# Rotary tables and softplus built before the input block arrives, and the sum of squares accumulated by TensorE, in a two-layer hybrid trunk

## The chip, the cores and the metric

One of the eight cores of a Trainium2 chip runs the whole program. The metric is the device time of one execution in microseconds; lower is better. Where an engine is named, PE is TensorE, DVE is VectorE, ACT is ScalarE, POOL is GpSimd and SP is SyncE, which here only issues transfers.

## The reference

Two layers over a sequence of 256 positions and 1024 channels. What the change touches is the start of a layer and three small things that depend on no activation:

```python
def rmsnorm(x, g):
    y = xf * lax.rsqrt(jnp.mean(xf * xf, axis=-1, keepdims=True) + EPS)
    return (y * g.astype(jnp.float32)).astype(x.dtype)
...
mod = c_act @ ada_w + ada_b
shift, scale, gate = jnp.split(mod, 3, axis=-1)
h = rmsnorm(x, norm_g) * (1.0 + scale[:, None]) + shift[:, None]
z = h @ w_in
...
log_a = -LRU_C * r * jax.nn.softplus(-lam.astype(jnp.float32))
...
ang = pos.astype(jnp.float32)[:, :, None] * inv
cos, sin = jnp.cos(ang), jnp.sin(ang)
...
q = rope(rmsnorm(b_q.reshape(shp), qn_g[:, None, :]), pos) * (HEAD_DIM ** -0.5)
k = rope(rmsnorm(b_k.reshape(shp), kn_g[:, None, :]), pos)
```

So h needs the whole of x (for the mean of squares) and the modulation vectors; the cosines and sines need only positions and a list of frequencies, and softplus only a parameter vector.

## The kernel before

The activations stay in SBUF. The weights are streamed: each layer is a list of units of 384 to 512 KB, and `load_next` issues one transfer per unit from SP's queue into one of six `raw` buffers. ACT copies a unit to the reduced-precision tile `whi` (L223), DVE makes the remainder `wlo` (L224), and PE forms three products per block: whi by the high part of h, wlo by it, and whi by the low part of h (L789 to L791 and L777 to L779 for the first units, L797 to L799 for the others). There are four `whi` and four `wlo` buffers.

At the start of layer 0 the modulation matrix also streams in, as sixteen tiles of 512 KB (`ada_...` and some `raw`). DVE reduces each of them against `crow`, the conditioning row spread over all partitions (L325). `crow` itself is made on the way: DVE computes `cact` from `c` and puts it on the diagonal of eight blocks (`diag`, L309), PE multiplies these by a matrix of ones (L313), ACT copies the result from PSUM (L314).

The statistics of x go as follows. `stats_start` squares x on ACT in four pieces (L372); DVE adds the four pieces to one (L375, L376); PE multiplies the two halves of that by ones (L379), which sums over partitions. `rstd_full` takes the logarithm on ACT (L341), the exponential of minus one half of it (L345), and refines that on DVE (L346 to L348). Then, for each of eight channel tiles j, DVE forms `tmp` (L357), ACT the high part `hhi` (L359) and DVE the low part `hlo` (L360).

The first sixteen units of a layer (q, k and v of the first pair of heads, and the gate bg, four each) are computed as one group; the prediction calls this the first group. Its results stay in PSUM until DVE and ACT have read them: for q and k, L552, L554 and L556 for each of two halves t. After it come units of one column block, the first of them ax and ag in turn (L797 to L799), which need the PSUM buffers that q and k have filled.

The order of instructions on each engine is set when the program is built, by a scheduler that takes the dependences, the order of the code and its own estimate of durations; `issue_after` adds a dependence by hand. Once built, every engine executes its own list strictly in order. Each activation function belongs to a table that ACT must have loaded; where the next one needs another table, the build puts a load of it ahead (ACT_TABLE_LOAD). L301 asks by hand for a table that holds both logarithm and exponential.

Of the kernel before, what the change touches and what calls it, by code (L numbers as in the profile page):

```python
# [10 lines left out]
F32 = mybir.dt.float32  # L11
# [3 lines left out]
ALU = mybir.AluOpType  # L15
# [3 lines left out]
D, S, L, P = 1024, 256, 2, 128  # L19
# [107 lines left out]
def hybrid_trunk(ctx: ExitStack, tc: tile.TileContext, ws, ada, vec, gates, a2, qkg, c_t, x_t, pos, inv, eye,  # L127
# [109 lines left out]
    SY.dma_start(out=c_sb, in_=c_t)  # L237
    SY.dma_start(out=eye_sb, in_=eye)
    for i in range(2):
        SY.dma_start(out=x_sb[:, 4 * i:4 * i + 4], in_=x_t[:, 4 * i:4 * i + 4])  # L240
    SY.dma_start(out=vec_sb, in_=vec)

# [20 lines left out]
    att_sb = one.tile([P, 3, P], F32, name="att_sb")  # L263
    G.memset(att_sb, 0.0)

    def load_after(key, *pairs):
# [101 lines left out]
    def stats_start():  # L368
        sq = []
        for i, tag in enumerate(("cv", "csg", "co", "bv")):  # L370
            t = two.tile([P, 2, S], F32, name="sq", tag=tag, bufs=1 if i < 3 else 2)
            A.activation(t, x_sb[:, 2 * i:2 * i + 2], AF.Square)  # L372
            sq.append(t)
            if i % 2:
                V.tensor_tensor(sq[i - 1], sq[i - 1], t, ALU.add)  # L375
        V.tensor_tensor(sq[0], sq[0], sq[2], ALU.add)  # L376
        ps = xps()
        for j in range(2):
            T.matmul(ps[:, 0:S], ones, sq[0][:, j], start=(j == 0), stop=(j == 1))  # L379
        return ps  # L380
# [50 lines left out]
    def rope_tables(l):  # L431
        gq = two.tile([P, 2, 3, 64], F32, name="gq", tag="pr", bufs=2)
        load_after(None if l else ("sy", "a", 7), (gq, qkg[l].partition_broadcast(P)))
        ct = one.tile([P, 2, 2, 3, 64], F32, name="ctab", tag="ctab")
# [514 lines left out]


    sts = stats_start()
    rstd = rstd_full(sts)
# [3 lines left out]

    def tables():
        a, v = cur["h_last"]
        with tc.issue_after(a), tc.issue_after(v):
            load_after(("sy", "a", 3), (pos_sb, pos), (inv_sb, inv.partition_broadcast(P)))  # L960
            angles()
            rope_tables(0)

    def small():
        a, v = cur["h_last"]
        with tc.issue_after(a), tc.issue_after(v):
            softplus()
        V.tensor_scalar(vec_sb[:, :, V_ON:V_ON + 2], vec_sb[:, :, V_ON:V_ON + 2], 0.5, None, ALU.mult)

    sts = layer(0, h, {2: tables, 15: load_small, 16: small})  # L970


# [98 lines left out]
```

## Time and profile before

| what | us |
|---|---|
| three runs | 910.75, 912.31, 912.46 |
| median | 912.31 |
| profiled execution | 912.47 |
| its span, first to last instruction | 910.7 |

The profiled execution lies 0.16 us above the median, and 1.8 us of its time lie outside the span. In the span PE is busy 96%, DVE 74%, ACT 58% and POOL 19%. All times below are microseconds from the start of the span. The start of the program is another regime than the rest: PE first gets to the layer's products at 20.41 us.

### The profile page before, as it was taken

Reading aid. Unit: us, or ns where it says so; the run is one execution under the profiler, and the core shown is the slowest. Engines: PE = TensorE matmul, PEld = TensorE weight load, DVE = VectorE, ACT = ScalarE, POOL = GpSimd, SP = SyncE. Lnnn points to the kernel's source line nnn. Section 1 sums busy time; section 2 is a strip of 40 time slices with the busy share of each in tenths; the row PEclk is TensorE's granted clock in tenths of the full one; section 3 lists DMA queues with packets and bytes.
Section 4 is the critical chain, followed back from the end, with each engine's and each line's share of the span. In section 5 each row is a group of like instructions: output and inputs, shape, how many; then the busy total and the mean of one; then the engine's idle time right before and its main releaser. Section 6 shows DMA issues by size and latency. Waiting matters only on the chain.

```text
span 910.7 us, 16407 instructions
## 1 busy us (share of the span) xinstructions
PE 872.9 (96%) x6340; PEld 825.3 (91%) x6340; DVE 673.0 (74%) x1115; ACT 532.0 (58%) x897; POOL 175.1 (19%) x160
## 2 busy tenths in 40 slices
PE   3989999999999999999999999989999999999998
PEld 3978999999988888999889999989999988899998
DVE  6998898669666667666775888986896666656674
ACT  4376976686644554634454689666874545554451
POOL 0026365124000110100030525551330001000000
PEclk9999999999999999999999999999999999999999
DMA  9884456446765666676655544563667565455651
GB/s 328 317 279 139 145 165 207 132 136 201 240 189 191 202 212 205 208 238 206 224 152 160 177 145 145 179 195 109 190 206 232 160 190 163 150 173 185 188 163 47
DMA packets 52111, 170.16 MB, mean 187 GB/s; under 512 B 6240, under 2 KB 8160, under 8 KB 52032
## 3 DMA queue, kind: packets, MB, share of 16 engines
q1 hardware_dynamic: 51216, 167.04, 57.7%
q10 hardware_dynamic: 672, 1.87, 0.7%
q8 instruction: 50, 0.82, 0.4%
q0 software_dynamic: 144, 0.20, 0.2%
q14 instruction: 29, 0.24, 0.1%
HBM read 168.23 MB, written 1.05 MB: 186 GB/s over the span
## 4 chain that ended last, share of the span: by engine, by line
PE 57%; DVE 18%; DMA 10%; issue 7%; ACT 5%; POOL 3%; SPq 0%; DVEq 0%; ACTq 0%
PE mm L797 10%; PE mm L799 10%; PE mm L798 10%; DMA raw<-in_ada_dram 8%; DVE wlo L224 7%; PE mm L791 6%; PE mm L790 6%; PE mm L789 6%; PE xps L172 1%; ACT whi L223 1%; POOL ss L560 1%; PE xps L168 1%; DVE raw L325 1%; DVE rb L554 1%; DVE ra L552 1%
## 5 line engine op out<-in xcount | busy, mean ns | idle before, releaser
L224 DVE TENSOR_TENSOR wlo<-raw,whi 128x1024 fp32r<-128x1024 f32 (+2 forms) x288 | 335.6, 1173 | 86.9 <-ACT whi L223 85.5
L223 ACT CAST whi<-raw 128x1024 fp32r<-128x1024 f32 (+2 forms) x288 | 280.2, 977 | 189.5 <-PE mm L798 123.6
L797 PE MATMUL mm<-hhi,whi 128*128 128x256 f32 x768 | 217.8, 284 | 3.3 <-DVE rb L554 3.2
L799 PE MATMUL mm<-hhi,wlo 128*128 128x256 f32 x768 | 216.6, 282 | 3.1 <-DVE wlo L224 3.1
L798 PE MATMUL mm<-hlo,whi 128*128 128x256 f32 x768 | 216.0, 281 | 0.0
L789 PE MATMUL mm<-whi,hhi 128*128 128x384 f32 (+2 forms) x480 | 170.9, 361 | 7.2 <-ACT hhi L359 6.5
L790 PE MATMUL mm<-wlo,hhi 128*128 128x384 f32 (+2 forms) x480 | 173.0, 362 | 1.4 <-DVE wlo L224 1.2
L791 PE MATMUL mm<-whi,hlo 128*128 128x384 f32 (+2 forms) x480 | 169.1, 358 | 0.5 <-DVE hlo L360 0.5
L797 PEld LDWEIGHTS mm<-hhi,whi 128*128 128x128 f32 x768 | 144.6, 188 | 5.3 <-ACT tmp L847 3.6
L799 PEld LDWEIGHTS mm<-hhi,wlo 128*128 128x128 f32 x768 | 144.5, 188 | 4.3 <-DVE wlo L224 3.7
L798 PEld LDWEIGHTS mm<-hlo,whi 128*128 128x128 f32 x768 | 144.8, 189 | 0.4
L789 PEld LDWEIGHTS mm<-whi,hhi 128*128 128x128 f32 x480 | 93.4, 195 | 15.3 <-ACT hhi L359 7.9
L790 PEld LDWEIGHTS mm<-wlo,hhi 128*128 128x128 f32 x480 | 93.9, 196 | 9.1 <-DVE wlo L224 2.8
L325 DVE CUSTOM_DVE_ANT_0 raw<-raw,crow,vec_sb 128x1024 f32<-128x1024 f32 x38 | 48.7, 1283 | 70.7 <-DMA raw<-in_ada_dram 70.7
L791 PEld LDWEIGHTS mm<-whi,hlo 128*128 128x128 f32 x480 | 92.7, 194 | 7.2 <-DVE hlo L360 0.8
L797 PE MATMUL mm<-yhi,whi 128*128 128x256 f32 x320 | 89.9, 281 | 2.1 <-DVE mg L939 2.1
L798 PE MATMUL mm<-ylo,whi 128*128 128x256 f32 x320 | 89.3, 279 | 0.0
L799 PE MATMUL mm<-yhi,wlo 128*128 128x256 f32 x320 | 89.2, 279 | 0.0
L797 PEld LDWEIGHTS mm<-yhi,whi 128*128 128x128 f32 x320 | 60.4, 189 | 3.1 <-DVE mg L939 2.3
L799 PEld LDWEIGHTS mm<-yhi,wlo 128*128 128x128 f32 x320 | 60.2, 188 | 0.8 <-DVE mrg L905 0.8
L798 PEld LDWEIGHTS mm<-ylo,whi 128*128 128x128 f32 x320 | 60.1, 188 | 0.0
L698 POOL TENSOR_TENSOR at_hl<-att_sb,at_hl 128x384 fp32r<-128x384 f32 x8 | 8.8, 1096 | 207.1 <-ACT at_hl L697 207.1
(236 smaller groups left out, 1408.0 us busy)
## 6 DMA issues: line engine op xcount, KB each, us to landing
raw<-in_ws_dram SPq DMA_DIRECT2D x192, 512.0 KB, 4.0
raw<-in_ws_dram SPq DMA_DIRECT2D x88, 384.0 KB, 3.2
raw<-in_ada_dram SPq DMA_DIRECT2D x38, 512.0 KB, 4.5
raw<-in_ws_dram SPq DMA_DIRECT2D x8, 400.0 KB, 5.4
g_raw<-in_gates_dram ACTq DMA_DIRECT2D x3, 512.0 KB, 4.9
x_sb<-in_x_t_dram SPq DMA_DIRECT2D x2, 512.0 KB, 6.7
ada_yhi<-in_ada_dram SPq DMA_DIRECT2D x2, 512.0 KB, 7.9
ada_ylo<-in_ada_dram SPq DMA_DIRECT2D x2, 512.0 KB, 9.1
```

Source lines behind the costliest of these rows:

```text
L168: seen[0] = T.matmul(*a, **k).ins
L172: seen[0] = T.transpose(*a, **k).ins
L223: A.copy(hi, r)
L224: V.tensor_tensor(lo, r, hi.bitcast(F32), ALU.subtract)
L325: V.tensor_tensor_reduce(w, w, crow2, 1.0, b, ALU.mult, ALU.add, a if i == 0 else m)
L552: V.tensor_tensor(ra.rearrange("p (g s) d -> p g s d", g=3), z4, ctab[l][:, i, t].unsqueeze(2).to_broadcast(bc), ALU.mult)
L789: T.matmul(o, ah, wh, start=(k == 0), stop=False)
L790: T.matmul(o, ah, wl, start=False, stop=False)
L791: T.matmul(o, al, wh, start=False, stop=(k == KT - 1))
L797: T.matmul(ps[:, 0:S], hi[:, a:b], xh[:, k], start=(k == 0), stop=False)
L798: T.matmul(ps[:, 0:S], hi[:, a:b], xl[:, k], start=False, stop=False)
L799: T.matmul(ps[:, 0:S], lo[:, a:b], xh[:, k], start=False, stop=(k == nk - 1))
```

## The change

The sum of squares loses its three additions on DVE; PE accumulates eight products instead of two. Positions, frequencies and the gains of layer 0 (`g0`, a tile that shares the buffer of `pt1`) are loaded from ACT's queue at the very start, and no longer from SP's queue among the weights; the parameter vector `vec` is loaded ahead of x. `angles`, `rope_tables(0)`, `softplus` and the halving of one parameter stand in the code ahead of `stats_start`; before, they were held behind the h tiles by `issue_after`.

```diff
--- before.py
+++ after.py
@@ -236,9 +236,9 @@
     inv_sb = one.tile([P, 32], F32, name="inv_sb")
     SY.dma_start(out=c_sb, in_=c_t)
     SY.dma_start(out=eye_sb, in_=eye)
+    SY.dma_start(out=vec_sb, in_=vec)
     for i in range(2):
         SY.dma_start(out=x_sb[:, 4 * i:4 * i + 4], in_=x_t[:, 4 * i:4 * i + 4])
-    SY.dma_start(out=vec_sb, in_=vec)
 
     tiles = []
     for tag, n in (("yhi", 2), ("ylo", 2), ("hraw", 2), ("ya", 1), ("sga", 1), ("la", 1), ("big2", 1)):
@@ -262,6 +262,10 @@
     V.memset(hpi, float(np.pi / 2))
     att_sb = one.tile([P, 3, P], F32, name="att_sb")
     G.memset(att_sb, 0.0)
+
+    g0 = one.tile([P, 2, 3, 64], F32, name="g0", tag="pt1")
+    for t, s in ((pos_sb, pos), (inv_sb, inv.partition_broadcast(P)), (g0, qkg[0].partition_broadcast(P))):
+        A.dma_start(out=t, in_=s)
 
     def load_after(key, *pairs):
 
@@ -371,12 +375,9 @@
             t = two.tile([P, 2, S], F32, name="sq", tag=tag, bufs=1 if i < 3 else 2)
             A.activation(t, x_sb[:, 2 * i:2 * i + 2], AF.Square)
             sq.append(t)
-            if i % 2:
-                V.tensor_tensor(sq[i - 1], sq[i - 1], t, ALU.add)
-        V.tensor_tensor(sq[0], sq[0], sq[2], ALU.add)
         ps = xps()
-        for j in range(2):
-            T.matmul(ps[:, 0:S], ones, sq[0][:, j], start=(j == 0), stop=(j == 1))
+        for j in range(KT):
+            T.matmul(ps[:, 0:S], ones, sq[j // 2][:, j % 2], start=(j == 0), stop=(j == KT - 1))
         return ps
 
 
@@ -429,8 +430,10 @@
     ctab, stab = {}, {}
 
     def rope_tables(l):
-        gq = two.tile([P, 2, 3, 64], F32, name="gq", tag="pr", bufs=2)
-        load_after(None if l else ("sy", "a", 7), (gq, qkg[l].partition_broadcast(P)))
+        gq = g0
+        if l:
+            gq = two.tile([P, 2, 3, 64], F32, name="gq", tag="pr", bufs=2)
+            load_after(None, (gq, qkg[l].partition_broadcast(P)))
         ct = one.tile([P, 2, 2, 3, 64], F32, name="ctab", tag="ctab")
         st = one.tile([P, 2, 2, 3, 64], F32, name="stab", tag="stab")
         V.tensor_scalar(gq[:, 0], gq[:, 0], 0.125, None, ALU.mult)
@@ -948,26 +951,17 @@
         yield 0
 
 
+    angles()
+    rope_tables(0)
+    softplus()
+    V.tensor_scalar(vec_sb[:, :, V_ON:V_ON + 2], vec_sb[:, :, V_ON:V_ON + 2], 0.5, None, ALU.mult)
     sts = stats_start()
     rstd = rstd_full(sts)
     h = h_alloc(0)
     hhi["h"] = h
     cur["rstd"], cur["h"] = rstd, h
 
-    def tables():
-        a, v = cur["h_last"]
-        with tc.issue_after(a), tc.issue_after(v):
-            load_after(("sy", "a", 3), (pos_sb, pos), (inv_sb, inv.partition_broadcast(P)))
-            angles()
-            rope_tables(0)
-
-    def small():
-        a, v = cur["h_last"]
-        with tc.issue_after(a), tc.issue_after(v):
-            softplus()
-        V.tensor_scalar(vec_sb[:, :, V_ON:V_ON + 2], vec_sb[:, :, V_ON:V_ON + 2], 0.5, None, ALU.mult)
-
-    sts = layer(0, h, {2: tables, 15: load_small, 16: small})
+    sts = layer(0, h, {15: load_small})
 
 
     rstd = rstd_full(sts, 4)
```

On DVE, at the start of the program (cact, diag and the sums before; the same stretch up to the first modulation tile), the list before is:

```order
L303 TENSOR_SCALAR cact<-cact 128x8
L304 RECIPROCAL cact<-cact 128x8
L305 TENSOR_TENSOR cact<-cact,c_sb 128x8
L309 TENSOR_TENSOR diag<-eye_sb,cact 128x1024
L375 TENSOR_TENSOR sq<-sq 128x512
L307 TENSOR_SCALAR vec_sb<-vec_sb 128x2x8
L968 TENSOR_SCALAR vec_sb<-vec_sb 128x2x2
L375 TENSOR_TENSOR sq<-sq 128x512
L376 TENSOR_TENSOR sq<-sq 128x512
L325 ISA ada_yhi,acc<-ada_yhi,crow,vec_sb 128x1024
```

In the changed program (line numbers of the changed file) the part of the same list from the scaling of the gains `g` to `diag` is:

```order
L439 TENSOR_SCALAR g_124<-g_124 128x192
L422 SCALAR_TENSOR_TENSOR an_158<-an_159,an_158 128x64
L307 TENSOR_SCALAR cact<-cact 128x8
L393 TENSOR_SCALAR spl_185<-spl_184 128x16
L422 SCALAR_TENSOR_TENSOR an_158<-an_159,an_158 128x64
L308 RECIPROCAL cact<-cact 128x8
L394 RECIPROCAL spl_185<-spl_185 128x16
L424 TENSOR_SCALAR an_158<-an_158 128x64
L309 TENSOR_TENSOR cact<-cact,c_sb 128x8
L395 TENSOR_TENSOR spl_185<-spl_185,spl_184 128x16
L426 SCALAR_TENSOR_TENSOR an_159<-an_158 128x64
L313 TENSOR_TENSOR diag<-eye_sb,cact 128x1024
```

cact and diag now stand behind the first use of the gains, and the additions of sq are gone.

On ACT, at the same place (squares, crow, the two steps of the root), before and then changed:

```order
L301 ACT_TABLE_LOAD
L302 ACTIVATE cact<-c_sb 128x8
L372 ACTIVATE sq<-x_sb 128x512 x4
L314 COPY crow<-xps 128x512 x2
L341 ACTIVATE rs_y<-xps,epsc 128x256
L345 ACTIVATE rs_y<-rs_y 128x256
L223 CAST whi<-raw 128x800
```

```order
L306 ACTIVATE cact<-c_sb 128x8
L392 ACTIVATE spl_184<-spl_184 128x16
L425 ACT_TABLE_LOAD
L425 ACTIVATE sn<-an_158 128x2x32
L427 ACTIVATE cs<-an_159,hpi 128x64
L376 ACTIVATE sq<-x_sb 128x512 x4
L318 COPY crow<-xps 128x512 x2
L345 ACT_TABLE_LOAD
L345 ACTIVATE rs_y<-xps,epsc 128x256
L349 ACT_TABLE_LOAD
L349 ACTIVATE rs_y<-rs_y 128x256
L223 CAST whi<-raw 128x800
```

The table of the sine is loaded ahead of the squares, so the logarithm and then the exponential each have a load ahead of them.

On DVE, behind the root (the last step of `rstd_full`, then weights and h tiles), before and then changed:

```order
L348 SCALAR_TENSOR_TENSOR rs_y<-rs_q,rs_y 128x256
L224 TENSOR_TENSOR wlo<-raw,whi 128x800
L357 SCALAR_TENSOR_TENSOR tmp<-x_sb,mod,rs_y 128x256 x2
L224 TENSOR_TENSOR wlo<-raw,whi 128x768 x2
L360 SCALAR_TENSOR_TENSOR hlo<-tmp,mod,hhi 128x256 x2
```

```order
L352 SCALAR_TENSOR_TENSOR rs_y<-rs_q,rs_y 128x256
L224 TENSOR_TENSOR wlo<-raw,whi 128x800
L224 TENSOR_TENSOR wlo<-raw,whi 128x768 x2
L361 SCALAR_TENSOR_TENSOR tmp<-x_sb,mod,rs_y 128x256 x2
L224 TENSOR_TENSOR wlo<-raw,whi 128x1024
```

Two more of the weight remainders now stand ahead of the first h tile.

## Rows read from the trace of the kernel before

**Rows 1.** Busy time by stretch: length, then each engine's busy us (count), PE clock, DMA.

```profile
20.00:62.40 42.40, 40.45 (x241) 38.54 (x241) 42.06 (x92) 20.84 (x32) 2.83 (x2) 1.00 0.90 331
62.40:77.30 14.90, 10.33 (x79) 9.43 (x80) 14.90 (x31) 9.91 (x22) 10.56 (x10) 1.00 0.50 152
77.30:96.00 18.70, 18.70 (x155) 18.10 (x154) 14.53 (x25) 15.34 (x26) 6.98 (x6) 1.00 0.41 116
```

**Rows 2.** Timeline of PE: start, us, line, tiles, count, idle before it.

```profile
4.61 3.78 PE L313 MATMUL xps<-diag,ones 128*128 128x128 f32 x16 [4.61 <-DVE diag L309]
11.89 2.04 PE L379 MATMUL xps<-sq,ones 128*128 128x256 f32 x4 [3.50 <-DVE sq L376]
20.41 0.70 PE L789 MATMUL mm<-whi,hhi 128*128 128x400 f32 x1 [6.47 <-ACT hhi L359]
...
25.04 0.35 PE L790 MATMUL mm<-wlo,hhi 128*128 128x400 f32 x1
...
62.36 0.36 PE L797 MATMUL mm<-hhi,whi 128*128 128x256 f32 x1
```

**Rows 3.** Timeline of ACT around the root.

```profile
10.20 1.05 ACT L314 COPY crow<-xps 128x512 f32<-128x512 f32 x2
13.97 0.47 ACT L341 ACTIVATE rs_y<-xps,epsc 128x256 f32<-128x256 f32 x1 [2.72 <-PE xps L379]
14.48 0.42 ACT L345 ACTIVATE rs_y<-rs_y 128x256 f32<-128x256 f32 x1
```

**Rows 4.** Timeline of DVE up to the first h tiles.

```profile
3.33 1.23 DVE L309 TENSOR_TENSOR diag<-eye_sb,cact 128x1024 f32<-128x1024 f32 x1
...
11.05 0.69 DVE L376 TENSOR_TENSOR sq<-sq 128x512 f32<-128x512 f32 x1
11.66 1.28 DVE L325 CUSTOM_DVE_ANT_0 ada_yhi<-ada_yhi,crow,vec_sb 128x1024 f32<-128x1024 f32 x1
...
18.09 0.42 DVE L348 SCALAR_TENSOR_TENSOR rs_y<-rs_q,rs_y 128x256 f32<-128x256 f32 x1
18.43 0.98 DVE L224 TENSOR_TENSOR wlo<-raw,whi 128x800 fp32r<-128x800 f32 x1
19.33 0.88 DVE L357 SCALAR_TENSOR_TENSOR tmp<-x_sb,mod,rs_y 128x256 f32<-128x256 f32 x2
```

**Rows 5.** Timeline of DVE, angles and tables among the first group's work.

```profile
52.47 0.19 DVE L427 TENSOR_SCALAR sn<-sn 128x64 f32<-128x64 f32 x1
...
54.82 0.62 DVE L440 TENSOR_TENSOR ctab<-gq,cs 128x192 f32<-128x192 f32 x2
...
56.97 1.22 DVE L224 TENSOR_TENSOR wlo<-raw,whi 128x1024 fp32r<-128x1024 f32 x1
58.10 1.51 DVE L360 SCALAR_TENSOR_TENSOR hlo<-tmp,mod,hhi 128x256 fp32r<-128x256 f32 x1
...
61.20 0.55 DVE L552 TENSOR_TENSOR ra<-mm,ctab 128x384 f32<-128x384 f32 x1
...
76.78 0.54 DVE L554 TENSOR_TENSOR rb<-mm,stab 128x384 f32<-128x384 f32 x1
```

**Rows 6.** DVE by line, 59.5 to 77.3: busy us, mean ns | idle before.

```profile
L398 DVE SCALAR_TENSOR_TENSOR spl<-spl,spl 128x16 f32<-128x16 f32 x7 | 2.0, 288 | 0.0
```

**Rows 7.** Waits of PE, 62 to 78: us in total, times, longest.

```profile
PE mm L797 <- DVE rb L554: 3.2, 2, 2.6
```

**Rows 8.** Transfers: queue, count, KB, us from issue to landing; then SP's third issue.

```profile
gq<-in_qkg_dram ACTq DMA_DIRECT2D x1, 192.0 KB, 5.6
eye_sb<-in_eye_dram SPq DMA_DIRECT2D x1, 64.0 KB, 2.0
...
1.63 0.90 SPq L240 DMA_DIRECT2D x_sb<-in_x_t_dram  x2
```

**Rows 9.** Timeline of ACT, a table load and what follows it.

```profile
50.38 1.28 ACT L424 ACT_TABLE_LOAD   x1
51.67 0.26 ACT L424 ACTIVATE sn<-an 128x64 f32<-128x64 f32 x1
```

## The prediction

> **What bounds the kernel now.** I read the view by stretches first, because the change touches only the first 80 us of 911. From 20 to 62.4 us DVE works 42.06 of 42.4 us, and from 62.4 to 77.3 it works all of 14.9 us, while PE idles 4.6 of those 14.9; from 77.3 on PE is full (18.70 of 18.70) and DVE is not [rows 1]. So DVE sets the pace up to 77 us and PE behind it. That PE is busy from 20 to 62 does not mean that it is at its peak: 144 products of 384 or 400 columns, which start 0.18 us apart once PE is fast, and 96 of 256 columns, 0.12 us apart, make 36.9 us; the first group takes 41.95 us, from 20.41 to 62.36 [rows 2].
>
> Then I read the timelines of the start, engine by engine. PE spreads the conditioning row from 4.61 on, as soon as diag is made (3.33 plus 1.23) [rows 2, 4]. ACT copies crow at 10.20, when its squares are done, and is through at 11.25 [rows 3]. DVE adds squares until 11.74 and takes the first modulation tile at 11.66 [rows 4]. The sum over partitions ends at 13.93 [rows 2], logarithm and exponential at 14.9 [rows 3]; DVE finishes the root at 18.5, since it puts modulation tiles between, then does one weight remainder and the first tmp (19.33) [rows 4], and PE gets its first h at 20.41 [rows 2].
>
> In the second stretch the wait to see is PE's for `rb`, 3.2 us in two [rows 7]: the next units need PSUM that DVE has not read yet. That reading starts at 61.20 (first L552) and ends at 77.32 (fourth L554), 16.1 us of DVE without a pause [rows 5].
>
> **The change, part by part.**
>
> *Work taken out of the busy stretch.* The tables are eight multiplications from 54.82 to 56.97, 2.15 us [rows 5]. The angles and the scaling of the gains are twelve small instructions, the last 0.19 us long [rows 5]; as they overlap their neighbours I count 0.13 each, 1.6 us. Together 3.75 us of DVE ahead of the last hlo, which ends at 59.6 [rows 5]. Softplus is nineteen small ones; the seven at L398 alone are busy 2.0 us [rows 6]. I count 1.6 us of it between 61.20 and 77.32, by the mean of L398 less the overlap; the rest lies ahead of 61.20 or behind, where DVE has room. The three additions of squares are worth at most 0.4 us: the modulation tile behind them could not start before crow, 11.25 instead of 11.66 [rows 3, 4].
>
> *What it costs at the start.* Here the new order of DVE counts: cact and diag stand behind the first use of the gains. The gains are the third transfer on ACT's queue; SP's third is issued at 1.63, so I put it at 1.6 [rows 8]. Landing is not shown for this place: from below 2.0 us, as eye early in the program; from above 5.6, as the same tensor from the same queue in layer 1 [rows 8]. I take the middle, 3.8, so it lands at 5.4 (3.6 to 7.2). Then the scaling (0.2), ten small ones (1.3) and diag (1.23): diag ends at 8.1 instead of 4.56. The sixteen passes of L313 take 3.78 [rows 2], to 11.9, and the second crow copy 0.5 [rows 3], to 12.4, 1.15 later than before. The angles, tables and softplus behind diag (about 4.3 us) lie under that wait for PE and ACT, and cost nothing; if crow came at 11.25 again, 1.1 us of them would show.
>
> *The sum on PE.* Eight products instead of two are sixteen passes instead of four. Four take 2.04 us from 11.89 [rows 2]; at that rate sixteen take 7.6. PE ran at the lower of its two levels (1.2 and 2.4 GHz) there: a product of 400 columns takes 0.70 at 20.41 and 0.35 at 25.04 [rows 2]. In the new order PE goes from crow to the sum without a pause, busy since 8.1, and at 20.41 it became fast within 4.6 us of starting; but its 3.78 us from 4.61 brought no speed. So between 3.8 (all fast) and 7.6 I take 4.5: the sum ends at 16.4.
>
> *The table loads.* The sine's table pushes out the one that held logarithm and exponential, and the new list loads one for each. The logarithm's load lies in ACT's wait for the sum. The exponential's cannot: 0.47, then a load of 1.28 [rows 3, 9], then 0.42: 18.6. Four modulation tiles on DVE from 12.4 at 1.28 plus small ones end at 18.3, so DVE is just ready; its four steps of 0.3 to 0.4 end at 19.95 instead of 18.5, 1.45 later. ScalarE: Activation LUTs, of the Trainium skill, section "What ACT_TABLE_LOAD costs", says that a switch of table costs 1.28 us and a drain of 1.38 besides. The trace disagrees about the drain: the sine starts at 51.67, when its load of 1.28 from 50.38 is over [rows 9]. With the drain the first h would be late by 1.4 us more, and the sum below 1.4 us smaller.
>
> *First product.* Three remainders (0.90, 0.87, 0.87) instead of one stand ahead of tmp, so 1.74 us more: tmp 0.4 and the high part 0.5 behind them, first product at 23.5 instead of 20.41, 3.1 late.
>
> *Does PE make up for it?* Before, the group took 41.95 for 36.9 us of products and about 1.7 lost at the lower level, so 3.3 us were waits. Now DVE needs 41.1 less 3.75 from the root to the last hlo, so that ends at 57.3 instead of 59.6, ahead of PE: PE sets the end. I leave 1.0 us of waits, since DVE is ahead by only one or two instructions at each h tile: 23.5 + 36.9 + 1.7 + 1.0 = 63.1, against 62.36. Up to here the change has lost 0.7 us.
>
> *The stretch behind.* q is complete 3.1 us before the group's end in the new order (26 products of 256 columns at 0.12): 60.0. DVE has no backlog then, where softplus held it until 61.20 before. From first L552 to fourth L554 its list is 14.9 us: four readings at 1.39 (the last without its reduction), six remainders at 1.14, and 3.1 us of smaller ones. So 74.9 against 77.32: **2.4 us gained**, although the first product is 3.1 late. Behind it PE is full and the streams wait for buffers, not for the clock on the wall, so the gain lasts. 912.47 - 2.4 = 910.1 for the profiled execution; beside the median, 912.31, it would be 909.9. I say 910.0 and count the other cases from 912.4 too.
>
> *At no cost.* The three small transfers leave SP's queue, so weights are issued earlier, but the DMA engines are 0.90 busy in this stretch [rows 1] and the same bytes go ahead of them on another queue: 0, at best 0.5. PE's later start hides weights that come later; without that cover the same 0.5 is lost. x is about 0.5 to 1 us later behind vec and the gains; its squares end by about 11.2, under the wait for diag.
>
> **Rivals.**
>
> *The sum stays at the lower level.* It takes 7.6 instead of 4.5, so PE starts on h at 26.6 and 0.7 us are lost in all, 913.1. For it: 3.78 us of the same kind of product brought no speed at 4.61 [rows 2]. Against: now they go on without a pause. It decides when the sum takes over 6.9 us. If the gains also land at 7.2, 1.8 more, it is 914.9: slower beyond what can be told, which is 0.2%, 1.8 us.
>
> *The gain goes elsewhere.* DVE's reading may wait for something else (ACT's copies, buffers), or the later units, whose attention now comes about one unit later on PE, wait again: then only what a shorter DVE list gives directly is left, about 1 us less than the start costs or gains: 911.5 to 913. For it: from 62 to 77 ACT works 9.91 of 14.9 us [rows 1], so it is no idle helper.
>
> *The gains land early.* At 3.6 diag is no limit; squares and crow are, and the root ends at 19.0; without the 1.0 us of waits that is 4.4 in all, 908.0. Against: mask and x fill the same DMA engines then.
>
> *ACT has to run empty at a switch of table.* Then each load on the path costs a gap besides its 1.28. One load is on the path here, and if the gap is as long as the activation ahead of it, 0.5 us [rows 3], the time is 910.5. No load in this trace shows one: the next instruction starts 0.01 us behind the load of rows 9. The page named above has such a rule, and by its figure, an estimate, the time is 911.4.
>
> **How the numbers follow.** Forecast (1 to 4.5 us gained) 0.47, of which 0.06 too small to tell; sum at the lower level 0.20, of which 0.13 slower beyond 0.2% (with late gains, or a stall more) and 0.07 too small; gain goes elsewhere 0.16, of which 0.14 too small and 0.02 slower; early landing 0.05; ACT empty at a switch 0.03, too small to tell; what I have not seen 0.09, of which 0.03 faster, 0.02 too small and 0.04 slower. That makes faster 0.49, same 0.32, slower 0.19. The range goes from 907.5, the early landing with half a microsecond besides, to 914.3, which holds the sum at the lower level and leaves out its worst case with late gains. The forecast's own range is 907.9 to 911.4.
>
> **What would show it.** In the new profile: diag ending near 8.1 with DVE idle ahead of the gains; sixteen passes at L380 ending near 16.4; two table loads around L345 and L349, the second without a gap behind; first product near 23.5; DVE with pauses before 60; PE's idle time from the group's end to 77 down by 3 us. Wrong would be: a sum past 19, a first product past 26, or PE idle again for `rb` as long as now.

## The result: slower by 0.66%

The changed kernel takes 917.78 us (median of four runs, 917.38 to 918.2), the kernel before 912.38 in the same session (four runs, 910.75 to 913.44). The ratio is 1.0066, with a 95% interval from 1.0052 to 1.0079. The profiled execution took 917.38 us and its span is 915.6.

The timeline of DVE over the start of the changed kernel (start and duration in us, line, output and inputs, count, idle time before it) answers to [rows 4]:

```profile
4.52 0.39 DVE L415 TENSOR_SCALAR an<-inv_sb,an 128x32 f32<-128x32 f32 x2 [1.73 <-DMA inv_sb<-in_inv_dram]
8.21 0.18 DVE L311 TENSOR_SCALAR vec_sb<-vec_sb 128x16 f32<-128x16 f32 x1 [3.30 <-DMA vec_sb<-in_vec_dram]
...
9.30 0.16 DVE L307 TENSOR_SCALAR cact<-cact 128x8 f32<-128x8 f32 x1
...
10.16 1.22 DVE L313 TENSOR_TENSOR diag<-eye_sb,cact 128x1024 f32<-128x1024 f32 x1
...
11.56 1.16 DVE L443 TENSOR_TENSOR ctab<-g,cs 128x192 f32<-128x192 f32 x4
...
15.88 1.28 DVE L329 CUSTOM_DVE_ANT_0 ada_yhi<-ada_yhi,crow,vec_sb 128x1024 f32<-128x1024 f32 x1 [0.24 <-ACT crow L318]
...
22.18 0.42 DVE L352 SCALAR_TENSOR_TENSOR rs_y<-rs_q,rs_y 128x256 f32<-128x256 f32 x1
22.52 2.72 DVE L224 TENSOR_TENSOR wlo<-raw,whi 128x800 fp32r<-128x800 f32 x3
25.16 0.88 DVE L361 SCALAR_TENSOR_TENSOR tmp<-x_sb,mod,rs_y 128x256 f32<-128x256 f32 x2
```

The wait to see is the one of 3.30 us for `vec`. Its use at L311 stands ahead of cact in DVE's list, so cact, which ACT has ready at 3.63, is taken up by DVE only at 9.30, diag ends at 11.38 instead of 4.56, and the first modulation tile starts at 15.88 instead of 11.66. PE and ACT of the same stretch answer to [rows 2, 3]:

```profile
11.44 3.78 PE L317 MATMUL xps<-diag,ones 128*128 128x128 f32 x16 [11.44 <-DVE diag L313]
15.01 3.85 PE L380 MATMUL xps<-sq,ones 128*128 128x256 f32 x16
26.23 0.70 PE L792 MATMUL mm<-whi,hhi 128*128 128x400 f32 x1 [7.37 <-ACT hhi L363]
```

```profile
15.26 0.59 ACT L318 COPY crow<-xps 128x512 f32<-128x512 f32 x1 [1.12 <-PE xps L317]
15.86 1.28 ACT L345 ACT_TABLE_LOAD   x1
18.91 0.47 ACT L345 ACTIVATE rs_y<-xps,epsc 128x256 f32<-128x256 f32 x1 [1.76 <-PE xps L380]
19.40 1.28 ACT L349 ACT_TABLE_LOAD   x1
20.69 0.42 ACT L349 ACTIVATE rs_y<-rs_y 128x256 f32<-128x256 f32 x1
```

The sum of sixteen passes is fast, the first table load is hidden in ACT's wait, the second is not. The first product comes at 26.23 instead of 20.41. Now the stretches, which answer to [rows 1] (first the group, then up to the fourth unit behind it, then on; busy time and count of PE, PEld, DVE, ACT, POOL; granted clock, DMA share, GB/s):

```profile
20.00:66.10 46.10, 38.99 (x240) 38.29 (x241) 41.56 (x73) 21.43 (x35) 3.24 (x3) 0.93 0.86 313
66.10:79.90 13.80, 9.76 (x76) 8.93 (x74) 13.80 (x21) 9.60 (x20) 8.57 (x9) 1.00 0.57 163
79.90:96.00 16.10, 16.05 (x129) 15.54 (x130) 10.80 (x19) 11.87 (x21) 5.96 (x6) 1.00 0.41 124
```

DVE is no longer full in the group. The time taken from it has become idle time, just ahead of the first reading of q (timeline of DVE, answers to the end of [rows 5]):

```profile
59.17 1.22 DVE L224 TENSOR_TENSOR wlo<-raw,whi 128x1024 fp32r<-128x1024 f32 x1
63.65 0.56 DVE L555 TENSOR_TENSOR ra<-mm,ctab 128x384 f32<-128x384 f32 x1 [3.27 <-ACT sqq L550]
...
65.05 4.18 DVE L224 TENSOR_TENSOR wlo<-raw,whi 128x1024 fp32r<-128x1024 f32 x3
...
79.27 0.54 DVE L557 TENSOR_TENSOR rb<-mm,stab 128x384 f32<-128x384 f32 x1
```

DVE waits 3.27 us for q, which PE finishes late because it began late. From first `ra` to the end of the fourth `rb` it is 16.16 us, as before (16.12), although softplus is gone from it: six remainders stand there instead of five, and three of them take 4.18 us, 1.39 each, where they took 1.21.

Against the kernel before, the changed one is 5.82 us late at its first product, 3.77 at the end of the first group, 2.64 at the fourth unit behind it (79.95 instead of 77.31), 4.18 at the ninth (159.79 instead of 155.61), and 4.91 at the last product. Between the fourth unit and the ninth PE waits for more than before (waits of PE from 80.5 to 157 us, us in total, times, longest; changed kernel):

```profile
PE mm L793 <- DVE wlo L224: 1.7, 2, 1.0
PE xps L172 <- DVE ro L568: 0.4, 1, 0.4
```

The kernel before has neither between its fourth unit and 157 us, and one other:

```profile
PE xps L505 <- ACT g_hi L291: 0.7, 1, 0.7
```

So 2.1 us of waits stand against 0.7, which makes up 1.4 of the 1.54 us by which the lateness grows there. A further wait, 1.54 us for `t1t`, ends at 79.95, where the fourth unit starts, and is part of the 2.64.

### The profile page after: what moved, and what is told of

Read it like the earlier page. It is cut to its first block, busy times and chain, and to the rows that moved or that the text cites. A ratio compares the mean times of both kernels' runs of the same rounds, so it can differ in the third digit from the quotient of the medians.

```text
span 915.6 us, 16433 instructions
## 1 busy us (share of the span) xinstructions
PE 872.8 (95%) x6352; PEld 828.5 (90%) x6352; DVE 671.1 (73%) x1112; ACT 533.4 (58%) x898; POOL 178.6 (20%) x160
## 4 chain that ended last, share of the span: by engine, by line
PE 61%; DVE 15%; DMA 10%; issue 6%; ACT 6%; POOL 3%; DVEq 0%; SPq 0%; ACTq 0%
PE mm L800 11%; PE mm L802 11%; PE mm L801 11%; DMA raw<-in_ada_dram 7%; DVE wlo L224 6%; PE mm L794 6%; PE mm L792 6%; PE mm L793 6%; ACT whi L223 2%; PE xps L172 2%; POOL ss L563 1%; DMA g_raw<-in_gates_dram 1%; PE xps L168 1%; DVE ra L555 1%; DVE rb L557 1%
## 5 line engine op out<-in xcount | busy, mean ns | idle before, releaser
L802 PE MATMUL mm<-hhi,wlo 128*128 128x256 f32 x768 | 218.8, 285 | 0.4 <-DVE wlo L224 0.4
L801 PE MATMUL mm<-hlo,whi 128*128 128x256 f32 x768 | 218.4, 284 | 0.0
L800 PEld LDWEIGHTS mm<-hhi,whi 128*128 128x128 f32 x768 | 147.7, 192 | 6.0 <-ACT whi L223 1.8
L802 PEld LDWEIGHTS mm<-hhi,wlo 128*128 128x128 f32 x768 | 147.6, 192 | 1.6 <-DVE wlo L224 1.0
L801 PEld LDWEIGHTS mm<-hlo,whi 128*128 128x128 f32 x768 | 147.7, 192 | 0.5
```

The costliest lines, as they stand in the source:

```text
L800: T.matmul(ps[:, 0:S], hi[:, a:b], xh[:, k], start=(k == 0), stop=False)
L801: T.matmul(ps[:, 0:S], hi[:, a:b], xl[:, k], start=False, stop=False)
L802: T.matmul(ps[:, 0:S], lo[:, a:b], xh[:, k], start=False, stop=(k == nk - 1))
```

## Experiments

Twelve kernels ran. Theory A was that the late start, by DVE's wait for `vec`, is the loss; B that the sum on PE is; C that the time is lost behind 60 us, whatever the start does; D, formed after the first four, that two chains of the same length end in the root. The kernels ran in five rounds, beside the kernel before on the same chip (its medians: 912.83, 912.29 and 912.40 us in the three sessions). The start of the first product, of the first and fourth unit behind the group and of the ninth are from each kernel's one profile; in seven of these profiles (PE sum alone, diag first, start kept, tables on POOL, late start, loads alone, tables early) a stretch of 3.41 us at the lower clock level (granted clock 0.5) lies between 70 and 88 us. Where PE is busy it costs half of its length, at most 1.7 us, which is in their ninth unit, and for kernels 1, 3, 6, 8 and 9 in their fourth too. In kernels 8 and 10 another such stretch lies inside the group. The others have none between 32 us and their ninth unit.

| kernel | first product | first unit | fourth | ninth | median | ratio, 95% |
|---|---|---|---|---|---|---|
| before | 20.41 | 62.36 | 77.31 | 155.61 | 912.38 | |
| changed | 26.23 | 66.13 | 79.95 | 159.79 | 917.78 | 1.0066 [1.0052, 1.0079] |
| 1 PE sum alone | 22.70 | 64.56 | 79.92 | 157.74 | 915.03 | 1.0011 [0.9989, 1.0034] |
| 2 DVE sum | 26.03 | 66.43 | 80.22 | 160.04 | 918.43 | 1.0065 [1.0043, 1.0087] |
| 3 diag first | 27.04 | 67.16 | 83.27 | 161.20 | 917.77 | 1.0057 [1.0037, 1.0076] |
| 4 and one table | 26.26 | 66.61 | 81.29 | 160.18 | 918.42 | 1.0071 [1.0048, 1.0095] |
| 5 start kept | 21.20 | 64.96 | 76.18 | 154.12 | 911.69 | 0.9997 [0.9979, 1.0015] |
| 6 tables on POOL | 19.82 | 62.97 | 78.51 | 158.15 | 914.51 | 1.0028 [1.0010, 1.0046] |
| 7 remainders behind tmp | 24.76 | 66.39 | 80.20 | 159.97 | 918.37 | 1.0065 [1.0040, 1.0089] |
| 8 late start alone | 28.46 | 73.53 | 89.04 | 167.37 | 923.81 | 1.0120 [1.0096, 1.0144] |
| 9 loads alone | 24.29 | 66.28 | 82.64 | 159.31 | 914.88 | 1.0029 [1.0015, 1.0043] |
| 10 tables early | 22.65 | 65.98 | 80.95 | 159.88 | 918.13 | 1.0066 [1.0040, 1.0091] |
| 11 start kept, softplus late | 20.99 | 61.58 | 75.90 | 155.82 | 916.13 | 1.0044 [1.0027, 1.0060] |
| 12 changed again | 26.44 | 66.74 | 80.54 | 160.33 | 921.69 | 1.0099 [1.0075, 1.0123] |

Two things limit what the table can say. The changed kernel ran again only in the third session (kernels 9 to 12), where its median was 921.69 and not 917.78; so kernels 2 to 5 and 7 are set against a changed kernel of another session. And every edit had the build order the lists anew, also far behind the place of the edit. In the traces, from the first reading of q on, the lists of DVE, ACT and POOL are entry by entry those of the kernel before only in kernel 1. In kernels 2, 7, 11 and 12 they are those of the changed kernel (the steps of softplus apart), and kernel 4 has those of kernel 3. The changed kernel's differ from those of the kernel before between 64 and 144 us, and each of the others has lists of its own there.

**1. The sum on PE alone** (against the kernel before)

```diff
-            if i % 2:
-                V.tensor_tensor(sq[i - 1], sq[i - 1], t, ALU.add)
-        V.tensor_tensor(sq[0], sq[0], sq[2], ALU.add)
...
+        for j in range(KT):
+            T.matmul(ps[:, 0:S], ones, sq[j // 2][:, j % 2], start=(j == 0), stop=(j == KT - 1))
```

> The kernel before with one part of the change alone: PE accumulates eight products for the sum of squares, DVE adds nothing; tables, softplus and all loads stay as before. Theory A (the loss comes from the late start of DVE's list: the conditioning row waits for vec) expects little here: the sum ends at 15 to 17.5 us instead of 13.93, the first product of the layer comes 0 to 2 us late, and the time is 912.4 to 914. Theory B (the sum on PE is what costs) expects the first product after 24 us and a time of 915.5 or more.

The first product is 2.3 us late, a little more than the 2 expected. The median, 915.03, lies between the two forecasts, and the ratio is not told from 1, but its interval reaches to 0.34%: the sum is not the whole loss, and a part is not excluded. PE of this kernel, the sum's row:

```profile
10.63 6.69 PE L376 MATMUL xps<-sq,ones 128*128 128x256 f32 x16 [2.18 <-ACT crow L314]
```

The same sixteen passes take 6.69 us here, behind 2.18 us of idle time, and 3.85 in the changed kernel, where they follow the spreading of the conditioning row without a pause.

**2. The sum back on DVE** (against the changed kernel; the same lines the other way)

> The changed kernel with the sum of squares undone: DVE adds the pieces, PE does two products; loads, tables and softplus stay moved ahead. Theory A expects diag still at about 11.4 us, the sum over 1.5 to 2 us earlier than in the changed kernel, the first product at 24 to 25 us instead of 26.2 and a time of 916 to 917.5, still slower than before by 3.5 or more. Theory B expects the loss to go: 912.4 to 914.

The first product is 0.2 us earlier, not 1.2 to 2.2, and the time, 918.43, is not below the changed kernel's 917.78; theory A had expected 916 to 917.5. The sum itself ends 2.0 us earlier, but DVE reaches the root no sooner, since its four modulation tiles last until 20.7 here and 21.0 there. Both tests speak against theory B, by which the loss would have gone.

**3. Diag first on DVE** (against the changed kernel)

```diff
+    dg = V.tensor_tensor(diag, ...)
+    with tc.issue_after(dg.ins):
+        V.tensor_scalar(b1, b1, 1.0, None, ALU.add)
...
+    with tc.issue_after(dg.ins):
+        angles()
+        rope_tables(0)
+        softplus()
```

> The changed kernel, but DVE makes cact and diag first: everything that uses vec, positions, frequencies or gains is queued behind diag. Theory A expects diag to end near 5 us instead of 11.4, the second copy of crow near 14 instead of 15.9, the first product at 22.5 to 24 us instead of 26.2 and a time of 914 to 916. Theory C (the start is hidden again later; what costs is the stretch from 60 us on, where units come one behind the other) expects the time of the changed kernel within 1 us, 917 to 918.5, whatever the first product does.

Diag ends at 5.67 as expected, and the first product is not earlier but 0.8 later. The theory that the wait for `vec` was the one cause falls; the time, 917.77, is what theory C expected. DVE and PE of this kernel show why:

```profile
14.94 0.89 DVE L444 TENSOR_TENSOR ctab<-g,cs 128x192 f32<-128x192 f32 x3
...
16.64 1.28 DVE L330 CUSTOM_DVE_ANT_0 ada_yhi<-ada_yhi,crow,vec_sb 128x1024 f32<-128x1024 f32 x1
```

```profile
12.62 5.95 PE L381 MATMUL xps<-sq,ones 128*128 128x256 f32 x16 [3.12 <-ACT crow L319]
27.04 0.70 PE L793 MATMUL mm<-whi,hhi 128*128 128x400 f32 x1 [8.46 <-ACT hhi L364]
```

The tables now wait for a sine that stands on ACT behind the squares, the modulation tiles wait behind the tables, and most passes of the sum run at the lower level. With the wait at the front gone, the moved work itself fills the time.

**4. And one table load** (against kernel 3)

```diff
         A.activation(cs, k, AF.Sin, bias=hpi, scale=-1.0)
+            A.preload_act_table_set("natural_log_exp_and_others")
```

> The kernel of the third run, and right behind the cosines ACT loads the one table that holds logarithm and exponential, so that neither loads one behind the sum. Theory A expects root and first product 1.3 to 2.6 us earlier than in the third run (21 to 22 us) and a time 1 to 2 us below it, 913 to 914.5. Theory C expects no difference from the third run beyond 0.5 us.

The exponential ends at 18.01, 2.8 us earlier than in kernel 3, and the first product gains only 0.8, most of it because `vec` landed 0.7 earlier. DVE of this kernel:

```profile
15.87 1.28 DVE L330 CUSTOM_DVE_ANT_0 ada_yhi<-ada_yhi,crow,vec_sb 128x1024 f32<-128x1024 f32 x1
...
20.85 0.42 DVE L347 TENSOR_SCALAR rs_m<-xps 128x256 f32<-128x256 f32 x1
```

DVE takes up the root at 20.85 whatever ACT has done. So two chains end in the root: DVE's list, and sum with logarithm, load and exponential. In the changed kernel and in kernel 3 they are of nearly the same length (DVE takes up the root at 20.93 and 21.62, the exponential ends at 21.11 and 20.82), so that shortening one brings nothing.

**5. The start kept** (against the changed kernel, with one table load as in 4)

```diff
+    with tc.issue_after(dg.ins):
+        angles()
+    for e in range(2):
...
+        with tc.issue_after(cur["cs"]):
+            crc = A.copy(crow[:, 4 * e:4 * e + 4], ...)
+    with tc.issue_after(cur["an"]):
+        V.tensor_scalar(b1, b1, 1.0, None, ALU.add)
+        rope_tables(0)
+        softplus()
+    with tc.issue_after(cur["cs"]), tc.issue_after(crc.ins):
         sts = stats_start()
```

> The changed kernel with its start put in another order: DVE makes cact, diag and the angles first (they need no vec and no gains), then the tables, and softplus last; ACT does sine, cosine and one load of the table for logarithm and exponential before x lands, then crow, then the squares; three of the four first weight remainders and all modulation tiles from the fifth on stand behind the first tmp. Theory D (no single wait made the start late: DVE's list and the chain sum, logarithm, table load, exponential were both about 21 us long, so that only an edit to both brings it forward) expects crow by 11 us, root near 18 to 19 and the first product at 20 to 21.5 us instead of 26.2. The prediction's gain behind the start (less work on DVE from 50 to 77 us) then expects 908 to 911, below the kernel before. Theory C (that gain is not there, or is given back after 77 us) expects 912 to 914, as before, with the first product as early.

DVE and PE of this kernel:

```profile
5.45 0.16 DVE L412 CAST an<-pos_sb 128x2 f32<-128x2 int32 x1
...
8.51 0.61 DVE L444 TENSOR_TENSOR ctab<-g,cs 128x192 f32<-128x192 f32 x2
...
11.59 1.28 DVE L326 CUSTOM_DVE_ANT_0 ada_yhi<-ada_yhi,crow,vec_sb 128x1024 f32<-128x1024 f32 x1 [0.76 <-DMA ada_yhi<-in_ada_dram]
...
19.89 0.87 DVE L358 SCALAR_TENSOR_TENSOR tmp<-x_sb,mod,rs_y 128x256 f32<-128x256 f32 x2
```

```profile
21.20 0.70 PE L793 MATMUL mm<-whi,hhi 128*128 128x400 f32 x1 [4.58 <-ACT hhi L362]
```

With the loads, the sum on PE and, but for one table load, the work of the changed kernel, in another order, the first product is at 21.20, and the 5.4 us of loss are gone: 0.9997 of the kernel before. Theory D holds for the start: an edit to both chains brings it forward. That the start is all that the change cost does not follow, since the lists behind q are others than the changed kernel's too; kernel 11 separates the two. The kernel is not faster than before either, though its fourth unit starts 1.1 us earlier and the ninth 1.5, in spite of 3.41 us at the lower level from 76.73. What the prediction hoped to gain behind the start cannot be told from nothing.

**6. The tables on POOL** (against the kernel before)

```diff
-                V.tensor_tensor(ct[:, i, t]...
+                G.tensor_tensor(ct[:, i, t]...
```

> The kernel before with one edit: POOL and not DVE forms the eight products of the rotary tables, at the same place. This takes 2.2 us out of DVE's stretch from 50 to 60 us and leaves the start as it is. The prediction's gain expects the first read of q and k at 59 to 60 us instead of 61.2 and the time 1 to 2 us lower, 910.5 to 911.5. Theory C expects no gain, 912 to 913.5.

Neither came: the first reading of q is at 61.80 instead of 61.20, and the time is 0.28% longer. (The edit moves the eight products of layer 1 to POOL too.) DVE and POOL of this kernel:

```profile
53.62 2.90 DVE L224 TENSOR_TENSOR wlo<-raw,whi 128x768 fp32r<-128x768 f32 x2
56.44 0.82 DVE L360 SCALAR_TENSOR_TENSOR hlo<-tmp,mod,hhi 128x256 fp32r<-128x256 f32 x1
```

```profile
54.12 2.85 POOL L442 TENSOR_TENSOR stab<-gq,sn 128x192 f32<-128x192 f32 x2
```

While POOL works, a remainder pair (128x768 and 128x1024) takes 2.90 us where its two sizes take 0.95 and 1.22 in the kernel before, the low part 0.82 instead of 0.48, and steps of softplus up to 0.56 instead of 0.17. So this is not the clean test of the work's worth that it was meant to be: DVE paid for the tables without making them.

**7. Remainders behind tmp** (against the changed kernel)

```diff
+                    if 0 < it[1] < 4:
+                        st.enter_context(tc.issue_after(cur["t0"]))
                     V.tensor_tensor(lo, r, hi.bitcast(F32), ALU.subtract)
```

> The changed kernel, but the second to fourth weight remainder are queued behind the first tmp on DVE, as before the change, instead of ahead of it. The first product should come 1.5 to 1.8 us earlier, at 24.4 to 24.7 us. If the start's delay is what the time shows, 915.5 to 917; by theory C 917 to 918.5.

The first product comes 1.47 us earlier, and the group ends 0.26 us later. PE does not wait for these remainders (its one wait for any is 0.25 us, at 38.80). But the granted clock is 0.5 until 29.47 here and until 29.14 in the changed kernel, so that 4.7 us of the group instead of 2.9 run at the lower level, an estimated 0.9 us; and PE's waits in the group add up to 1.4 us instead of 0.9. With the changed kernel's lists behind q the time, 918.37, is what theory C expected. The 1.74 us that the prediction charged for the remainders are a shift of the first product, not of the group's end.

**8. A late start alone** (against the kernel before; three remainders and the modulation tiles from the fifth on held behind the first tmp)

```diff
-    V.tensor_tensor(diag, ...)
+    for _ in range(8):
+        dg = V.tensor_tensor(diag, ...)
```

> The kernel before, with a late start and nothing else: DVE makes diag eight times over (the same values), which moves it to about 13 us; the order of modulation tiles and remainders is held as before. No work leaves the stretch from 50 to 77 us. The first product should come at 25 to 27 us, as in the changed kernel. If the work taken out of that stretch is worth the 3.2 us that the changed kernel wins back between first product and 80 us, this one keeps its whole delay, at 917 to 919; if the kernel wins back a late start by itself there, 914.5 to 916, and the changed kernel gained nothing by the moved work.

It came out later than meant, with the first product at 28.46 (8.1 late), the fourth unit 11.7 late and the time 11.5 us longer. The late start is not won back. But it is not alone either: the lists behind the first product are not those of the kernel before. Its first low part of h stands behind four more modulation tiles, at 35.88, 7.4 us after the first product instead of 1.45, and PE waits for it:

```profile
36.41 0.67 PE L798 MATMUL mm<-whi,hlo 128*128 128x400 f32 x2 [3.26 <-DVE hlo L367]
```

Right behind that wait, from 36.90, PE has 3.41 us at the lower level. The two cover the 3.1 us by which the delay grows inside the group. The changed kernel loses 5.8 at the first product and has 2.6 left at the fourth unit. That the moved work is what wins this back, as cover for its own late start, is therefore argued and not shown.

**9. The loads alone** (against the kernel before)

```diff
+    SY.dma_start(out=vec_sb, in_=vec)
     for i in range(2):
         SY.dma_start(out=x_sb[:, 4 * i:4 * i + 4], in_=x_t[:, 4 * i:4 * i + 4])
-    SY.dma_start(out=vec_sb, in_=vec)
...
+    for t, s in ((pos_sb, pos), (inv_sb, inv.partition_broadcast(P)), (g0, qkg[0].partition_broadcast(P))):
+        A.dma_start(out=t, in_=s)
```

> The kernel before with the loads of the change alone: vec ahead of x, positions, frequencies and gains from ACT's queue at the very start; all computing stays where its code stood, the sum of squares on DVE. The order built from this puts the two small uses of vec ahead of cact on DVE. If vec, landing near 8, is what holds diag up, diag ends at 9.5 to 10 us instead of 4.6, crow comes at 13.5 to 14.5, the first product at 22.5 to 24 us and the time is 914 to 917, though no work was moved. If the transfers are without effect, as the prediction counted them, 911.5 to 913.

No work is moved by hand, and the first product is 3.9 us late, the time 2.5 us longer. (The lists behind q differ from those of the kernel before between 65 and 101 us.) DVE of this kernel, from its first real work on:

```profile
7.63 0.18 DVE L311 TENSOR_SCALAR vec_sb<-vec_sb 128x16 f32<-128x16 f32 x1 [6.61 <-DMA vec_sb<-in_vec_dram]
...
8.43 1.23 DVE L313 TENSOR_TENSOR diag<-eye_sb,cact 128x1024 f32<-128x1024 f32 x1
...
23.22 0.87 DVE L361 SCALAR_TENSOR_TENSOR tmp<-x_sb,mod,rs_y 128x256 f32<-128x256 f32 x2
```

Moving one transfer ahead of x let the scheduler put its user first on DVE, and everything waits 6.61 us for it. This is the part that the prediction counted at no cost. Together with kernel 3 it shows two causes of a late start, either of which is enough to make the first product 4 to 6.6 us late; kernel 5 takes both away.

**10. Tables early** (against the kernel before: loads from ACT's queue, angles and tables behind diag, one table load; `vec`, softplus and DVE's sum as before)

```diff
+    with tc.issue_after(dg.ins):
+        angles()
...
+    with tc.issue_after(cur["an"]):
+        rope_tables(0)
-            angles()
-            rope_tables(0)
```

> The kernel before, with angles and rotary tables alone moved into the time in which DVE and ACT wait for x (loads from ACT's queue, one table load behind the cosines); vec stays behind x, softplus and the sums of squares stay as before, and the order behind the root is held. First product at 21 to 22.5 us. The work taken out of 50 to 60 us is 3.75 us by the prediction's count: if it is worth that, first read of q and k at 58.5 to 60 us instead of 61.2 and 909 to 911; if nothing, 912.5 to 914.

The first product is 2.2 us late, a little more than expected, but q is first read at 64.27, later than before, and the time is 0.66% longer. The work taken out did not show as a gain, but here too the new list brings a wait of its own. The first low part of h comes 6.2 us after the first product instead of 1.45, and PE waits for it:

```profile
29.39 0.80 PE L799 MATMUL mm<-whi,hlo 128*128 128x400 f32 x2 [2.46 <-DVE hlo L364]
```

From 29.72 PE has 3.41 us at the lower level. Together that is more than the 1.4 us by which the group is longer than before.

**11. The start kept, softplus late** (against kernel 5)

```diff
-        softplus()
...
+    def small():
+        a, v = cur["h_last"]
+        with tc.issue_after(a), tc.issue_after(v):
+            softplus()
...
+    sts = layer(0, h, {15: load_small, 16: small})
```

> The kernel of the fifth run (start reordered, everything moved, sum on PE), but softplus back at its old place behind the last h tile. Softplus, spread over the first h tiles, no longer stretches them, and lies in the stretch from 58 to 68 us again. By the prediction's count softplus is worth 1.6 us there: 911 to 913. If its pieces among the first tiles cost as much as they save, the same as the fifth run within 1 us.

Its profile is the best of all up to the fourth unit, 1.4 us ahead of the kernel before; at the ninth it is 0.2 behind, and the median is 0.44% longer, where 911 to 913 was expected. A lead at 76 us is lost by 156, and the waits of PE from 80 to 157 us show where; they are those of the changed kernel:

```profile
PE mm L794 <- DVE wlo L226: 1.7, 2, 1.0
PE xps L172 <- DVE ro L569: 0.5, 1, 0.5
```

The lists behind q are the changed kernel's, with softplus back in them, and five kernels with these lists (changed, 2, 7, 11, 12) take 79.8 to 79.9 us from the fourth unit to the ninth, the kernel before 78.3, whether the first product comes at 21 or at 26 us. So this part of the loss belongs to the lists and not to the start. In the times, beside each other on one chip: 912.40 before, 916.13 here, 921.69 the changed kernel again. Of the 9.3 us, 5.6 go with the start (the place of softplus is the other difference), and 3.7 stay although the start is early. By this comparison theory C holds for that part and theory D for the larger one. Where in the program the 3.7 us lie is not shown: the profiled execution, 913.27, is the fastest of its twelve.

**12. The changed kernel again**

> The changed kernel once more, beside the others on the same chip. Time 916.5 to 919. If the 2.3 us that its first profile lost between 80 us and the end belong to the kernel, the second profile shows the delay against before grow from 2.6 at 80 us to 4 or more at 160 us again; if they are chance, it stays at 2 to 3.5 us.

The time, 921.69, lies above the expected 916.5 to 919, so the size of the loss is 0.7% in one session and 1.0% in the other. Up to the ninth unit the second profile repeats the first within 0.6 us, the waits of PE listed above included: the delay grows from 3.2 at the fourth unit to 4.7 at the ninth (2.6 and 4.2 in the first). So that growth belongs to the kernel. Behind it the two profiles of the same program part, from 0.1 us at 275 to 6.2 at the end.

## Why the prediction was wrong

It forecast 910.0 and faster; 917.78 was measured, outside the range, on the side that it gave 0.19. By its own steps, in the first profile:

*What it costs at the start* failed first and most. It put diag's end at 8.1, from gains landing at 5.4; diag ended at 11.38. That a small transfer holds diag up by its use on DVE's list was foreseen; its landing time was the term that was mis-sized, by 2.9 us. The transfer that DVE waited for was `vec`, whose move the prediction left at no cost, though its use, and steps of softplus that need it, stand ahead of diag in DVE's new list. The landing was mis-sized for both: the transfers view of the changed kernel (KB each, us from issue to landing) answers to [rows 8]:

```profile
g<-in_qkg_dram ACTq DMA_DIRECT2D x1, 192.0 KB, 6.7
vec_sb<-in_vec_dram SPq DMA_DIRECT2D x1, 102.0 KB, 6.5
eye_sb<-in_eye_dram SPq DMA_DIRECT2D x1, 64.0 KB, 3.1
```

Gains issued at 1.64 landed at 8.3, above the upper bound of 7.2: a bound taken from layer 1, 5.6 us, did not hold at the start. Without the uses of `vec` ahead of them the gains alone would have held diag almost as long: from their scaling at 9.00 to diag's end it is 2.38 us, so from 8.3 on, an estimate, until 10.7. Loads alone (9) show such a wait for `vec` by itself. That angles, tables and softplus behind diag cost nothing held in the changed kernel, where DVE still waits 0.24 us for crow; diag first (3) shows that it hung on diag being late: with the wait gone the first modulation tile stands behind them until 16.64, 1.8 us after crow's second copy, where the prediction allowed 1.1 us for that case.

*The sum on PE* was right in kind and better than sized: 3.85 us for 4.5, at the higher level from 15.5 on, so the rival of the lower level did not happen. It ended at 18.86 instead of 16.4 because it began late. Alone (1), behind 2.18 us of idle time, it took 6.69 us.

*The table loads* were right in size: one hidden, one behind the logarithm at 1.28, and no gap. The exponential starts at 20.69, 0.01 us behind the end of its load from 19.40. ScalarE: Activation LUTs, of the Trainium skill, section "What ACT_TABLE_LOAD costs", adds a drain of 1.38 us to a switch; this trace shows none, as before. That the second load is on the path was not borne out: DVE works without a pause from 15.88 past the root and takes up the exponential's result at 21.26, 0.15 us after its end, and in kernel 4, without that load, the first product gains little more than what `vec` gave.

*First product* at 23.5 became 26.23: diag was 3.3 us later than counted, and the four modulation tiles, 5.1 us instead of 5.9, gave some of it back; the sum was not on the path (2). Of the 1.74 us for the two remainders, kernel 7 showed that they move the first product and not the group's end.

*Does PE make up for it?* From first product to the group's end 39.6 us were predicted, 39.90 measured. This step holds: PE sets the end, and DVE's saved time lies idle.

*The stretch behind* was mis-sized by 1.9 us: q was there 0.6 us later than counted from the group's end, and 14.9 us of list (its terms add up to 15.0) were 16.16, because the six remainders took 8.1 us instead of 6.8. POOL is busy for 8.57 of the 13.8 us there, and kernel 6 shows that POOL's work can stretch DVE's; that it does so here is not shown, since POOL is busy for 10.56 of 14.9 us there in the kernel before [rows 1], where the five remainders between the readings took 1.21 or 1.22 each. With q at 63.65, the DVE time freed by softplus had already passed as a wait.

*That "the gain lasts"* failed too. The lateness at the fourth unit, 2.64, was 4.18 at the ninth (3.23 and 4.72 in the second profile), through waits for remainders that the kernel before does not have there; kernel 11, with the same lists and an early start, lost a lead of 1.4 us in the same stretch by the same waits. The lists behind 77 us came out in another order than before, and the prediction had no term for that.

So of the 7.3 us between the forecast for the profiled execution, 910.1, and the 917.38 measured, 2.7 are there at the first product, 0.3 come in the group, 1.9 up to the fourth `rb` and the rest behind it. Of the rivals, "the gain goes elsewhere" was nearest, but it started from a start that cost only 0.7.

What the change costs is thus shown in two parts: a start that is late by 5.8 us, which kernel 5 brings down to 0.8, and another order of the lists behind q, which loses 1.5 us up to the ninth unit whatever the start does. How the time divides between them rests on one comparison, of kernels 11 and 12.

Open: why kernel 5, with its start 0.8 us later than before and less work for DVE, is not faster, and where behind the ninth unit kernel 11 loses what its median shows. Within one session the runs of one kernel spread over up to 8.7 us (the kernel before beside kernels 1 to 4: 909.70 to 918.37), so differences under about 2 us in the stretch behind 160 us could not be followed. No kernel here is measurably faster than the one before.

## What to carry to other kernels

When a load is moved to the front, look first at which instruction uses it and what that instruction now stands in front of: on an engine that runs its list in order, an early user of a late transfer is a wait for everything behind it. Work moved "into a wait" is free only if its own inputs are there before the wait begins and every engine that it passes through is free then; angles in the idle time behind diag were free (5), tables that needed `vec`, gains and a sine were not (3). Taking work off an engine pays only while that engine sets the end: where the same edit delays another engine, the freed time comes back as idle time, 3.27 us here. And where a build orders the lists, an edit can change more than it says: before a kernel is called a test of one cause, its lists should be set beside those of the kernel it is compared with, to the end. Of the five experiments set against the kernel before (1, 6, 8, 9 and 10), that leaves the first.

## What the runs showed of the hardware

Small transfers at the very start are slow: 102 KB took 6.5 us and 64 KB 3.1 where the same 64 KB took 2.0 in the kernel before, with fewer transfers beside it [rows 8]. `vec` took 6.0 in the kernel with the loads alone, and 6.8 in the kernel before, issued behind x.

DVE and POOL slow each other: with POOL at the tables, DVE's steps took up to three times as long (0.56 instead of 0.17, 0.82 instead of 0.48), and two of POOL's products 2.85 us where later ones took 0.59 to 0.78 each. SBUF — State Buffer, of the Trainium skill, section "Who interferes with whom", says that the only contention is an exclusive lock on the port pair that DVE and GpSimd share; the rows of kernel 6 agree that both are held up, and do not show the port.

The same sixteen passes took 3.85 to 4.15 us directly behind other products (the changed kernel, 7 and 12), 3.72 behind 1.74 us of idle time (11), and 5.20 to 6.69 behind 2.2 to 3.1 us (1, 3, 4 and 5). The change's order gave PE its higher level at 15.5 us, and its wait of 7.37 us for h took the level away again, from 22.3 to 29.1 us.

One program does not keep its rhythm: two executions of the changed kernel agree within 0.6 us for 275 us and are 6.2 us apart at the end.
